# A hybrid encoder layer on one core: the second projection keeps its last input, lower weight parts stay in DRAM, the FFN weights get a memory of their own, and the last x1T store goes in four parts

## The chip, the cores and the metric

The kernel is one program on one core of a Trainium2 chip. The metric is the time of one execution on the device in microseconds (us); lower is better. The quoted time is the median of several executions.

## What is computed

One encoder layer over two requests of 256 and 2048 tokens (2304 in all) of width 1024, with shared weights, all in fp32. Cut to what matters:

```python
mod = silu(c) @ ada_w + ada_b                      # six vectors: sh1, sc1, g1, sh2, sc2, g2
h = rmsnorm(x, norm1_g) * (1 + sc1) + sh1
proj = h @ w_in                                    # 1024 -> 3*512 (hyena) + 3*512 (attention)
hy = hyena_mixer(proj[..., :1536], ...)            # short conv, two long convolutions by FFT,
                                                   # whose filters come from a small network
at = dilated_attention(proj[..., 1536:])           # 8 heads, three dilations, ALiBi
mix = concat([rmsnorm(hy, hy_out_g), rmsnorm(at, attn_out_g)]) @ w_out
x = x + g1 * mix                                   # x1
h = rmsnorm(x, norm2_g) * (1 + sc2) + sh2
gate = dwconv3(h @ ffn_w_gate, ...)                # 1024 -> 2816
x = x + g2 * ((gelu(gate) * (h @ ffn_w_up)) @ ffn_w_down)
return rmsnorm(x, final_g)
```

## The kernel before, in words

**Arithmetic.** An fp32 matmul is made of three matmuls in a shorter format: each operand is split into an upper part (a rounded copy, made by ScalarE) and a lower part (operand minus upper part, made by VectorE or GpSimd). `mm3` (L205) issues the three: upper weight by upper input (L208), upper weight by lower input (L209), lower weight by upper input (L210). All subtractions of this kind go through `sub`, so L203 stands for many tiles; they are told apart by their names. The input's parts are hThi and hTlo in the projections and hh and hl in the FFN, the weights' parts wihi and wilo there and whi and wlo here.

**Order of the work.** The stages are Python generators, and `weave` (L247) advances several of them by hand-set rates, so that one stage's matmuls stand among another's. Each engine then executes its own instructions in the order of issue. DMAs issued by SyncE (SP) stand in SP's queue in order, those issued by ScalarE in ScalarE's: a DMA that waits holds what is behind it in that queue. The program gives each DMA that SP and ScalarE issue one of eight completion counters, in turn, and a DMA waits until the one eight before it has landed.

**First projection** (`project`, L587, called from L1063). The tokens are walked in three passes of 768 own tokens (`OWN`, L477; with a few neighbours beside them, up to 772). For each pass twelve column blocks m = 0 to 11 of `w_in` are multiplied. `load_w` (L577) loads a block of 128 columns (wiraw, 512 KB, on SP, L580), casts its upper part on ScalarE (L583) and subtracts on VectorE. It does so in each pass again: the 36 block-steps load, cast and subtract 36 times. Raw, upper and lower part have two buffers each. After the matmuls ScalarE copies PSUM to the tile u (L627 or L629), a short convolution runs on GpSimd and VectorE (tile cv, L662), TensorE transposes the result (pjt, L601), and the tokens are stored by SP (L606). At block 6 of a pass `modulated` (L556) prepares the next pass's input: x is loaded on SP (L489), normed on VectorE (L519) and modulated on ScalarE and other engines (L553); at the start of the next pass `split` (L565) makes hThi (ScalarE, L571) and hTlo (VectorE).

This projection is woven with `filters` (L330): matmuls (fw, L432; fs, through `mm3`) make the filters' spectrum, VectorE forms F (L439), GpSimd forms flo and sums absolute values into acc (L454), and ScalarE's tile fae is stored on SP (d_fA, L421) 72 times. The filters end near 480 us, and the first projection runs on nearly alone until 555.

**Second projection** (L1088). The same function with m = 12 to 23 and no H given: it starts with `modulated` for pass 0, splits it, and does so again for passes 1 and 2. It is woven with the hyena convolutions. Attention's q and k of head 0 are first read after step 35 of the generator's 39 (L1097 to L1100).

**Output projection** (`output`, L1185). Blocks of 256 tokens; in each, eight column blocks m (PSUM tile om), whose results VectorE adds to x in the tile ox (L1215). At the block's end ScalarE's queue stores ox whole to x1T in DRAM (L1232, 1 MB). The previous block goes through `ffn_block` (L1236), which makes the FFN operands (tiles fV, fT) and stores them to opT in DRAM from ScalarE's queue (L1254 to L1256).

**FFN** (`output_ffn`, L1281). Both matrix products use a scheme with seven block products instead of eight; its operands are B11, T1, T2, B21, T3, B22 and T4. `operands` (L1322) loads them from opT on SP (tile hl, L1329, 289 KB each; two of the seven for the first half of the tokens are loaded ahead, beside the last output blocks), casts hh on ScalarE (L1330) and subtracts on VectorE or GpSimd. `weights7` (L1335) loads 1 MB of gate or up weights on SP (wraw, L1340), and makes the seven weight combinations from it, each with an upper part (ScalarE, L1346) and a lower part. `gate_up` runs for the two halves of the tokens; its results go to DRAM (tile cv of L1457, d_G). `down_sums` and `down_first` (L1468, L1498) prepare the down product's weights, `down` (L1520) computes it; its pool d_w holds the weights' parts dwl and dwh (L1551, L1552), and `down_first` leaves the first weights in the list W0.

**Memory.** Pools are stacked from both sides of each partition, and a pool opened where a closed one lay has its tiles wait for what was there, tile by tile (`reuse_waits="tile"`). The weights of `weights7`, `down_sums` and `down_first` lie in one pool, n_w (47,520 bytes of a partition: raw 16,384, upper 6,144, lower 6,144, the rest combinations and kept PSUM sums), which is opened after m_r, the pool of the output weights of blocks 0 to 2 (27,648 bytes), and the pools o_c and o_w of `output` are closed. The part of it that the change moves, raw and upper parts, makes 22,528 bytes.

Of the kernel before, what the change touches and what calls it, by code (L numbers as in the profile page):

```python
# [13 lines left out]
F32 = mybir.dt.float32  # L14
F32R = mybir.dt.float32r
# [6 lines left out]
P = 128  # L22
D = 1024
NT = 2304
# [165 lines left out]
class Hybrid:  # L190
# [383 lines left out]

    XB = 8

    def load_w(self, wp, src, k, tag, n=8, raws=3, bufs=2):  # L577
        nc = self.nc
        raw = wp.tile([P, 8, P], F32, tag="wraw", name=tag + "raw", bufs=raws)[:, :n]
        nc.sync.dma_start(out=raw, in_=src)  # L580
        hi = wp.tile([P, 8, P], F32R, tag="whi", name=tag + "hi", bufs=bufs)[:, :n]
        lo = wp.tile([P, 8, P], F32R, tag="wlo", name=tag + "lo", bufs=bufs)[:, :n]
        nc.scalar.copy(hi, raw)  # L583
        self.sub(nc.vector, lo, raw, hi)
        return hi, lo

    def project(self, hp, wp, w2, psp, ms, H=None):  # L587

        nc, a = self.nc, self.a
        pending = []  # L590

        def flush():
            while pending:
                pending.pop(0)()

        def to_tokens(src, dst, o0, o1, k):
            def go():
                for t0 in range(0, 6, 3):
                    ps = psp.tile([P, 512], F32, tag="pt", name="pjt", bufs=2)
                    for t in range(3):  # L600
                        nc.tensor.transpose(ps[:, t * P:(t + 1) * P], src[:, (t0 + t) * P:(t0 + t + 1) * P],  # L601
                                            self.ident)
                    if t0 == 0:
                        tt = wp.tile([P, 6, P], F32, tag="tt", name="tt", bufs=2)
                    nc.vector.tensor_copy(tt[:, t0:t0 + 3], ps[:, :3 * P].rearrange("p (t c) -> p t c", c=P))
                nc.sync.dma_start(out=dst[o0:o1].rearrange("(t p) c -> p t c", p=P)[:, :, k * P:(k + 1) * P], in_=tt)  # L606
            return go

        for p in range(3):
            if p == 0 and H is None:  # L610
                X = self.modulated(wp, 0)
            if p or H is None:
                H = [[], []]
                self.split(hp, X, H)
            yield
            o0, o1 = self.OWN[p]
            base = self.PASS[p][0][0]
            for m in ms:
                wh, wl = self.load_w(wp, a["w_in"][m], m, "wi", raws=2)
                u = wp.tile([P, 772], F32, tag="u", name="u", bufs=2)  # L620
                for (c0, n), hs in zip(self.PASS[p], H):
                    ps = psp.tile([P, 512], F32, tag="ps", name="pj")
                    for j in range(8):
                        self.mm3(ps[:, :n], wh[:, j], wl[:, j], hs[j][0], hs[j][1], j == 0, j == 7)
                    us = u[:, c0 - base:c0 - base + n]
                    if 12 <= m < 16:
                        nc.scalar.mul(us, ps[:, :n], -0.125)  # L627
                    else:
                        nc.scalar.copy(us, ps[:, :n])  # L629
                flush()  # L630
                src = u[:, o0 - base:o1 - base]
                if m < 12:
                    src = self.short_conv(w2, u, base, o0, o1, m)
                k = m % 4
                if 12 <= m < 20:
                    dst = self.qT if m < 16 else self.kT
                    nc.sync.dma_start(out=dst[k * P:(k + 1) * P, o0:o1], in_=src)
                else:
                    dst = self.tok[("hv", "x1", "x2", "", "", "av")[m // 4]]
                    pending.append(to_tokens(src, dst, o0, o1, k))  # L640
                yield
                if p < 2 and m == ms[2] and w2 is not None:
                    yield from self.input_rstd(wp, w2, psp, p + 1)
                if p < 2 and m == ms[5]:
                    X = self.modulated(wp, p + 1)
        flush()

    def short_conv(self, wp, u, base, o0, o1, m):
# [395 lines left out]
    def mixers(self):  # L1044
# [15 lines left out]
        H = [[], []]  # L1060
        for i in range(0, 8, 4):
            self.split(hp, self.modulate(X[i:i + 4], True), H)
        g = self.project(hp, wp, w2, ps, range(0, 12), H)  # L1063
        for x in (g, f, f, f):
            next(x)
        self.weave([[f, R["f"], 0], [g, R["p1"], 0]])
# [12 lines left out]
        with ExitStack() as st:  # L1079
            ap = self.pool(st, "ada2", side="left")  # L1080

            def rest():
                rows = self.ada_rows(ap)
                for i in (2, 3, 4, 5):
                    yield from self.ada_vector(i, ap, rows, 1)
                    self.ada_finish(i)

            g = self.project(hp, wp, None, ps, range(12, 24))  # L1088
            rs = rest()
            gw = [g, R["p2"], 0]  # L1090
            self.weave([h, [rs, R["ad"], 0], gw], until=rs)
# [93 lines left out]
    def output(self, psp, ap):  # L1185
# [3 lines left out]
        with ExitStack() as st:  # L1189
# [13 lines left out]
            for c0 in range(0, NT, 256):  # L1203
# [7 lines left out]
                for m in range(8):  # L1211
# [14 lines left out]
                    if m == 3 and last is not None:  # L1226
                        px, pacc, pc, pr = last
                        rs = wp.tile([P, 256], F32, tag="ors2", name="ors2", bufs=1)
                        self.rstd(psp.tile([P, 512], F32, tag="pr", name="rstd", bufs=1), [pacc], rs)
                        self.ffn_block(ap[2], px.rearrange("p (k j) t -> p k j t", k=2), rs, pc, pr, range(4))  # L1230
                    yield
                nc.scalar.dma_start(out=self.x1T[:, :, :, c0 // 2:c0 // 2 + P], in_=xe)  # L1232
                last = (xT, acc, c0, r)
            self.last = last[1:]

# [45 lines left out]
    def output_ffn(self, hy, mq, ow):  # L1281
        with ExitStack() as top, ExitStack() as s:
# [19 lines left out]
            for x in "hl":  # L1302
                for i in range(7):
                    self.hpool.setdefault((x, i), h2)
            psp = self.pool(top, "psB", bufs=8, space=PSUM)
            wp = self.pool(s, "n_w", side="right")
            gp = self.pool(s, "n_g", side="right")
            self.Gd = self.dr.tile([P, NF // 2, 7, NT // 2], F32, name="d_G")
# [26 lines left out]
    def weights7(self, wp, src):  # L1335

        nc = self.nc
        v = nc.vector
        raw = wp.tile([P, 2, 2, 4, P], F32, tag="wraw", name="wraw", bufs=2)
        nc.sync.dma_start(out=raw, in_=src)  # L1340
        A11, A12, A21, A22 = raw[:, 0, 0], raw[:, 0, 1], raw[:, 1, 0], raw[:, 1, 1]

        def parts(x, eng):
            hi = wp.tile([P, 4, P], F32R, tag="whi", name="whi", bufs=3)
            lo = wp.tile([P, 4, P], F32R, tag="wlo", name="wlo", bufs=3)
            nc.scalar.copy(hi, x)  # L1346
            self.sub(eng, lo, x, hi)
# [120 lines left out]
    def down_sums(self, wp, n):  # L1468
# [1 line left out]
        nc = self.nc  # L1470
        mp, q0 = n // 3, 4 * (n % 3)
        q1 = min(q0 + 4, NF // 2)
        raw = wp.tile([P, 2, 2, 4, P], F32, tag="wraw", name="sraw", bufs=2)[:, :, :, :q1 - q0]
        for r in range(2):
            nc.sync.dma_start(out=raw[:, r], in_=self.a["w_down"][mp, :, r, :, q0:q1])
        A11, A12, A21, A22 = raw[:, 0, 0], raw[:, 0, 1], raw[:, 1, 0], raw[:, 1, 1]
# [21 lines left out]
    def down_first(self, wp, T, W):  # L1498
# [7 lines left out]
            if q % 4 == 3:  # L1506
                yield
        yield
        raw = wp.tile([P, 2, 2, 4, P], F32, tag="wraw", name="draw", bufs=2).rearrange("p r k q m -> p (r k q) m")[:, :NQ]
        nc.sync.dma_start(out=raw, in_=self.a["w_down"][0, :, 0, 0])  # L1510
        yield
        yield
        for q0 in range(0, NQ, 4):
            k = min(4, NQ - q0)
            hi, lo = (wp.tile([P, 4, P], F32R, tag="w" + x, name="dw" + x, bufs=3)[:, :k] for x in ("hi", "lo"))
            nc.scalar.copy(hi, raw[:, q0:q0 + k])
            self.sub(nc.vector, lo, raw[:, q0:q0 + k], hi)
            W += [(hi[:, q], lo[:, q]) for q in range(k)]
# [168 lines left out]
```

## Time and profile before

| | |
|---|---|
| median of 3 runs | 3480.42 us (3474.23 to 3481.12) |
| profiled execution, its own time | 3475.7 us |
| span of that execution, first to last instruction | 3473.9 us |
| granted TensorE clock, mean of the span | 0.973 of full |
| instructions | 56,909 |

The profiled execution is one run, and every row further down comes from it. Engines are named as in the profile: PE is TensorE's matmuls, PEld its weight loads (which overlap PE), DVE is VectorE, ACT ScalarE, POOL GpSimd, SP SyncE; SPq and ACTq are the DMA queues of SyncE and ScalarE. "idle before" a group of instructions is the time its engine stood idle just ahead of them, with what ended that idle time behind an arrow. PEclk is the granted TensorE clock, 1.00 being 2.4 GHz and 0.50 being 1.2 GHz. Times in brackets such as 1904 to 1938 are us from the start of the span.

### The profile page before, as it was taken

Reading aid. Unit: us, or ns where it says so; the run is one execution under the profiler, and the core shown is the slowest. Engines: PE = TensorE matmul, PEld = TensorE weight load, DVE = VectorE, ACT = ScalarE, POOL = GpSimd, SP = SyncE. Lnnn points to the kernel's source line nnn. Section 1 sums busy time; section 2 is a strip of 40 time slices with the busy share of each in tenths; the row PEclk is TensorE's granted clock in tenths of the full one; section 3 lists DMA queues with packets and bytes.
Section 4 is the critical chain, followed back from the end, with each engine's and each line's share of the span. In section 5 each row is a group of like instructions: output and inputs, shape, how many; then the busy total and the mean of one; then the engine's idle time right before and its main releaser. Section 6 shows DMA issues by size and latency. Waiting matters only on the chain.

```text
span 3473.9 us, 56909 instructions
## 1 busy us (share of the span) xinstructions
PE 3256.6 (94%) x20926; PEld 3001.6 (86%) x20926; DVE 2459.5 (71%) x4233; ACT 1559.7 (45%) x2895; POOL 1279.4 (37%) x1018
## 2 busy tenths in 40 slices
PE   7988899989989998998898899999999999899998
PEld 4877788778867786777898899999999999899998
DVE  7988878777576667744886766776866667457657
ACT  4576753233245645455554433334433334344443
POOL 1487661133233423210544433334533335123222
PEclk9999999999999999999899999999999999999999
DMA  6454457777585867584676523445443224557555
GB/s 246 133 163 136 149 173 234 229 255 231 192 227 176 246 189 214 173 257 137 181 214 201 186 97 123 151 163 206 148 159 143 97 90 148 181 181 239 201 192 172
DMA packets 408910, 628.02 MB, mean 181 GB/s; under 512 B 29007, under 2 KB 232015, under 8 KB 402711
## 3 DMA queue, kind: packets, MB, share of 16 engines
q1 hardware_dynamic: 355472, 593.13, 52.6%
q10 hardware_dynamic: 52072, 28.40, 2.8%
q8 instruction: 166, 2.72, 0.3%
q0 software_dynamic: 1088, 2.85, 0.2%
q14 instruction: 112, 0.92, 0.1%
HBM read 419.03 MB, written 205.25 MB: 180 GB/s over the span
## 4 chain that ended last, share of the span: by engine, by line
PE 42%; DVE 5%; DMA 2%; issue 2%; ACT 1%; POOL 1%; SPq 0%; ACTq 0%; DVEq 0%; POOLq 0%
PE w L210 9%; PE w L208 9%; PE w L209 9%; PE fd L210 5%; PE fd L209 5%; PE fd L208 5%; DVE fT L1252 1%; DMA hl<-d_opT 0%; DMA d_x1T<-ox 0%; DVE ohy L1160 0%; DVE ox L1215 0%; PE om L208 0%; POOL oat L1146 0%; PE om L209 0%; PE om L210 0%
## 5 line engine op out<-in xcount | busy, mean ns | idle before, releaser
L208 PE MATMUL w<-hh,whi 128*128 128x288 f32 (+1 forms) x2464 | 735.6, 299 | 13.2 <-ACT whi L1346 8.4
L210 PE MATMUL w<-hh,wlo 128*128 128x290 f32 (+1 forms) x2464 | 733.5, 299 | 11.2 <-POOL wlo L203 7.0
L209 PE MATMUL w<-hl,whi 128*128 128x288 f32 (+1 forms) x2464 | 735.4, 299 | 2.7 <-DVE hl L203 2.7
L208 PEld LDWEIGHTS w<-hh,whi 128*128 128x128 f32 x2464 | 471.1, 191 | 14.5 <-ACT whi L1346 8.6
L210 PEld LDWEIGHTS w<-hh,wlo 128*128 128x128 f32 x2464 | 470.4, 191 | 13.2 <-POOL wlo L203 8.0
L209 PEld LDWEIGHTS w<-hl,whi 128*128 128x128 f32 x2464 | 472.7, 192 | 3.4 <-DVE hl L203 3.2
L208 PE MATMUL pj<-hThi,wihi 128*128 128x386 f32 (+1 forms) x1152 | 402.4, 350 | 12.9 <-ACT u L629 5.4
L209 PE MATMUL pj<-hTlo,wihi 128*128 128x386 f32 (+1 forms) x1152 | 399.3, 347 | 7.1 <-DVE hTlo L203 7.1
L210 PE MATMUL pj<-hThi,wilo 128*128 128x386 f32 (+1 forms) x1152 | 401.7, 349 | 0.0
L208 PE MATMUL fd<-hh,dwh 128*128 128x288 f32 x1210 | 360.3, 298 | 12.6 <-ACT dwh L1552 12.6
L210 PE MATMUL fd<-hh,dwl 128*128 128x288 f32 x1210 | 359.0, 297 | 0.0
L209 PE MATMUL fd<-hl,dwh 128*128 128x288 f32 x1210 | 357.9, 296 | 0.0
L208 PEld LDWEIGHTS pj<-hThi,wihi 128*128 128x128 f32 x1152 | 220.2, 191 | 28.3 <-issue 7.8
L208 PEld LDWEIGHTS fd<-hh,dwh 128*128 128x128 f32 x1210 | 230.0, 190 | 13.2 <-ACT dwh L1552 12.8
L209 PEld LDWEIGHTS pj<-hTlo,wihi 128*128 128x128 f32 x1152 | 220.6, 192 | 23.9 <-issue 9.7
L210 PEld LDWEIGHTS pj<-hThi,wilo 128*128 128x128 f32 x1152 | 219.9, 191 | 11.7 <-issue 7.5
L209 PEld LDWEIGHTS fd<-hl,dwh 128*128 128x128 f32 x1210 | 229.6, 190 | 0.4
L210 PEld LDWEIGHTS fd<-hh,dwl 128*128 128x128 f32 x1210 | 228.0, 188 | 0.1
L939 PEld LDWEIGHTS aOp<-aV,aPT 128*128 128x128 f32 x1408 | 184.3, 198 | 48.8 <-issue 18.4
L735 POOL TENSOR_TENSOR ht<-ht,ht 128x512 f32<-128x512 f32 x72 | 101.7, 1413 | 338.4 <-DVE ht L734 268.2
L203 POOL TENSOR_TENSOR wlo<-ws,whi 128x512 fp32r<-128x512 f32 x88 | 131.6, 1495 | 232.3 <-ACT whi L1346 225.4
L203 POOL TENSOR_TENSOR hl<-hl,hh 128x576 fp32r<-128x576 f32 (+1 forms) x66 | 116.1, 1766 | 264.6 <-ACT hh L1494 191.4
(298 smaller groups left out, 7950.1 us busy)
## 6 DMA issues: line engine op xcount, KB each, us to landing
hl<-d_G SPq DMA_DIRECT2D x154, 288.0 KB, 5.1
dwl<-d_S SPq DMA_DIRECT2D x59, 704.0 KB, 4.9
wiraw<-in_w_in SPq DMA_DIRECT2D x72, 512.0 KB, 4.6
d_G<-cv SPq DMA_DIRECT2D x42, 576.0 KB, 2.9
wraw<-in_w_gate SPq DMA_DIRECT2D x22, 1024.0 KB, 4.8
wraw<-in_w_up SPq DMA_DIRECT2D x22, 1024.0 KB, 4.9
adat<-in_ada_t SPq DMA_DIRECT2D x36, 512.0 KB, 5.6
d_fA<-fae SPq DMA_DIRECT2D x72, 256.0 KB, 2.5
```

The lines of the kernel that those rows point to most:

```text
L203: eng.tensor_tensor(out=lo, in0=x, in1=hi.bitcast(F32), op=ALU.subtract)
L208: mm(out, wh, xh, start=first, stop=False, skip_group_check=more)
L209: mm(out, wh, xl, start=False, stop=False, skip_group_check=more)
L210: mm(out, wl, xh, start=False, stop=last, skip_group_check=more)
L735: nc.gpsimd.tensor_tensor(out=t1, in0=t1, in1=t2, op=ALU.add)
L939: nc.tensor.matmul(po[:, i, hs], pe[:, hh, c], vt[:, x["v"] + c * x["vs"], hs], start=(c == 0), stop=(c == n - 1))
L1252: v.tensor_tensor(out=o, in0=x, in1=y, op=ALU.subtract)
```

## The change

It has four parts.

1. **Kept input.** `project` takes the input and the order of the passes. The first projection leaves its last split input (of pass 2) in `self.H`; the second starts with it and walks the passes as 2, 1, 0. So it modulates and splits two inputs instead of three.
2. **Lower weight parts in DRAM.** In its first pass the first projection stores each wilo to a DRAM tile (12 stores of 512 KB on SP, behind the subtraction). In passes 1 and 2 it loads wilo from there (24 loads of 512 KB on SP, issued right behind the raw load and the upper part's cast) instead of subtracting. The second projection still subtracts.
3. **A memory of their own.** Raw and upper parts of `weights7`, `down_sums` and `down_first` go to a new pool n_r, opened ahead of n_w; lower parts and the rest stay in n_w.
4. **The last x1T store.** In the last block of `output` x1T is stored by SP in four parts of 256 KB, one after each pair of column blocks; the other blocks keep ScalarE's whole store.

```diff
-    def load_w(self, wp, src, k, tag, n=8, raws=3, bufs=2):
+    def load_w(self, wp, src, k, tag, n=8, raws=3, bufs=2, kept=None, known=False):
         ...
         nc.scalar.copy(hi, raw)
-        self.sub(nc.vector, lo, raw, hi)
+        if known:
+            nc.sync.dma_start(out=lo.bitcast(F32), in_=kept)
+        else:
+            self.sub(nc.vector, lo, raw, hi)
+            if kept is not None:
+                nc.sync.dma_start(out=kept, in_=lo.bitcast(F32))
         return hi, lo

-    def project(self, hp, wp, w2, psp, ms, H=None):
+    def project(self, hp, wp, w2, psp, ms, H, passes):
         ...
-        for p in range(3):
-            if p == 0 and H is None:
-                X = self.modulated(wp, 0)
-            if p or H is None:
+        lows = self.dr.tile([len(ms), P, 8, P], F32, name=f"d_wlo{ms[0]}") if w2 is not None else None
+        for p, after in zip(passes, passes[1:] + (None,)):
+            if p != passes[0]:
                 H = [[], []]
                 self.split(hp, X, H)
+            self.H = H
             yield
             ...
-                wh, wl = self.load_w(wp, a["w_in"][m], m, "wi", raws=2)
+                wh, wl = self.load_w(wp, a["w_in"][m], m, "wi", raws=2, kept=None if lows is None else lows[m - ms[0]],
+                                     known=lows is not None and p != passes[0])
                 ...
-                if p < 2 and m == ms[2] and w2 is not None:
-                    yield from self.input_rstd(wp, w2, psp, p + 1)
-                if p < 2 and m == ms[5]:
-                    X = self.modulated(wp, p + 1)
+                if after is not None and m == ms[2] and w2 is not None:
+                    yield from self.input_rstd(wp, w2, psp, after)
+                if after is not None and m == ms[5]:
+                    X = self.modulated(wp, after)
 # mixers
-        g = self.project(hp, wp, w2, ps, range(0, 12), H)
+        g = self.project(hp, wp, w2, ps, range(0, 12), H, (0, 1, 2))
-            g = self.project(hp, wp, None, ps, range(12, 24))
+            g = self.project(hp, wp, None, ps, range(12, 24), self.H, (2, 1, 0))
 # output
+                    if c0 + 256 == NT and m % 2:
+                        nc.sync.dma_start(out=self.x1T[:, m - 1:m + 1, :, c0 // 2:c0 // 2 + P], in_=xe[:, m - 1:m + 1])
                     yield
-                nc.scalar.dma_start(out=self.x1T[:, :, :, c0 // 2:c0 // 2 + P], in_=xe)
+                if c0 + 256 < NT:
+                    nc.scalar.dma_start(out=self.x1T[:, :, :, c0 // 2:c0 // 2 + P], in_=xe)
 # output_ffn
+            self.rp = self.pool(s, "n_r", side="right")
             wp = self.pool(s, "n_w", side="right")
 # weights7, and the raw tiles of down_sums and down_first in the same way
-        raw = wp.tile([P, 2, 2, 4, P], F32, tag="wraw", name="wraw", bufs=2)
+        raw = self.rp.tile([P, 2, 2, 4, P], F32, tag="wraw", name="wraw", bufs=2)
         ...
-            hi = wp.tile([P, 4, P], F32R, tag="whi", name="whi", bufs=3)
+            hi = self.rp.tile([P, 4, P], F32R, tag="whi", name="whi", bufs=3)
             lo = wp.tile([P, 4, P], F32R, tag="wlo", name="wlo", bufs=3)
```

## Rows read from the trace of the kernel before

**Rows 1.** The page's first part: busy time of each engine, its share of the span, and its instructions.

```profile
PE 3256.6 (94%) x20926; PEld 3001.6 (86%) x20926; DVE 2459.5 (71%) x4233; ACT 1559.7 (45%) x2895; POOL 1279.4 (37%) x1018
```

**Rows 2.** The table by stage: the stretch and its length, then busy time (and instructions) of PE, PEld, DVE, ACT and POOL, the granted clock PEclk, the DMA engines' busy share, and the GB/s that they moved.

```profile
211.00:480.00 269.00, 243.31 (x1235) 216.22 (x1235) 234.24 (x241) 196.51 (x342) 210.74 (x140) 0.97 0.47 146
480.00:555.00 75.00, 72.56 (x410) 69.11 (x408) 59.15 (x70) 31.66 (x48) 26.13 (x16) 1.00 0.77 240
552.00:563.00 11.00, 7.58 (x29) 7.26 (x28) 10.06 (x14) 7.24 (x13) 0.00 (x0) 0.69 0.76 246
...
1904.00:1938.00 34.00, 20.02 (x95) 18.49 (x94) 20.84 (x22) 14.66 (x28) 14.88 (x12) 0.70 0.90 314
1938.00:2408.00 470.00, 468.85 (x3483) 468.29 (x3482) 330.61 (x485) 170.62 (x325) 178.45 (x146) 1.00 0.38 134
...
2938.00:2973.00 35.00, 17.60 (x108) 16.66 (x108) 24.72 (x32) 10.03 (x13) 13.55 (x11) 0.80 0.47 175
```

**Rows 3.** Instructions grouped by line, VectorE, 211 to 555: count, busy time, mean ns of one, then the idle time just before them and what ended most of it.

```profile
L439 DVE TENSOR_TENSOR F<-fw,fE 64x512 f32<-64x512 f32 x114 | 78.4, 688 | 26.7 <-POOL flo L203 16.5 <-PE fw L433 5.9 <-ACT fE L430 1.5
L203 DVE TENSOR_TENSOR wilo<-wiraw,wihi 128x1024 fp32r<-128x1024 f32 x25 | 41.7, 1670 | 0.8 <-ACT wihi L583 0.4
```

**Rows 4.** The same grouping, TensorE's matmuls, 211 to 480.

```profile
L209 PE MATMUL pj<-hTlo,wihi 128*128 128x386 f32 (+1 forms) x279 | 96.4, 346 | 5.6 <-DVE hTlo L203 5.6
L432 PE MATMUL fw<-W3s,Hh 128*128 128x512 f32 x55 | 23.6, 429 | 12.8 <-DVE F L439 12.7
L209 PE MATMUL fs<-flo,fkt 128*128 128x512 f32 x56 | 23.5, 419 | 2.0 <-POOL flo L203 2.0
L601 PE MATMUL pjt<-ident,cv 128*128 128x128 f32 x106 | 16.9, 283 | 3.7 <-DVE cv L662 3.7
```

**Rows 5.** The same grouping, GpSimd, 211 to 480.

```profile
L454 POOL TENSOR_TENSOR acc<-acc,fabs 128x512 f32<-128x512 f32 x60 | 92.9, 1549 | 28.7 <-ACT fabs L453 13.6 <-PE fw L433 10.9 <-DVE x L519 2.5
L203 POOL TENSOR_TENSOR flo<-F,fhi 128x512 fp32r<-128x512 f32 x56 | 90.5, 1621 | 3.3 <-ACT fhi L414 3.3
```

**Rows 6.** Waits of SP's DMA queue, 211 to 555: the line that waits and what it waited for, then us in total, times, and the longest in us.

```profile
SPq L421 <- ACT fae L420: 107.5, 38, 8.5
SPq L580 <- DVE wilo L203: 53.3, 22, 6.3
```

**Rows 7.** DMA issues, 211 to 555: destination and source, queue, count, KB each, and the median us from issue to landing.

```profile
d_fA<-fae SPq DMA_DIRECT2D x64, 256.0 KB, 2.9
wiraw<-in_w_in SPq DMA_DIRECT2D x25, 512.0 KB, 4.3
```

**Rows 8.** The table by stage for the instructions that touch the tile wilo alone: stretch, length, busy time (and count) of PE (the matmuls that read it or stand in its chains), PEld and DVE (the subtractions), then clock, DMA share and GB/s of the stretch.

```profile
211.00:480.00 269.00, 95.34 (x279) 53.43 (x279) 29.46 (x18) 0.97 0.47 146
480.00:555.00 75.00, 39.06 (x116) 21.62 (x115) 10.28 (x7) 1.00 0.77 240
```

**Rows 9.** Instructions grouped by line, ScalarE, 529 to 562 (the hand-over to the second projection).

```profile
L553 ACT ACTIVATE x<-x,mod,ga 128x386 f32<-128x386 f32 x14 | 9.0, 701 | 8.4 <-DVE x L519 8.4
L571 ACT CAST hThi<-x 128x772 fp32r<-128x772 f32 (+1 forms) x8 | 6.6, 837 | 1.2 <-PE pj L210 1.1
```

**Rows 10.** The same, VectorE, 529 to 562.

```profile
L519 DVE TENSOR_TENSOR x<-x,rs 128x772 f32<-128x772 f32 x8 | 8.5, 1087 | 0.0
L203 DVE TENSOR_TENSOR hTlo<-x,hThi 128x772 fp32r<-128x772 f32 (+1 forms) x8 | 8.0, 1027 | 0.0
```

**Rows 11.** The same, TensorE's matmuls, 480 to 562.

```profile
L208 PE MATMUL pj<-hThi,wihi 128*128 128x384 f32 (+1 forms) x121 | 42.7, 356 | 3.4 <-ACT u L627 3.4
```

**Rows 12.** The timeline of ScalarE's queue near the FFN's start: start in us, length in us, queue, line, what was issued.

```profile
1905.46 6.58 ACTq L1232 DMA_DIRECT2D d_x1T<-ox  x1
```

**Rows 13.** Waits of SP's DMA queue, 1860 to 1935, as in rows 6.

```profile
SPq L1340 <- PE om L210: 25.2, 2, 22.7
...
SPq L1329 <- DMA d_opT<-fT: 6.0, 1, 6.0
SPq L1329 <- DMA d_opT<-fV: 4.4, 1, 4.4
...
SPq L1329 <- DMA d_x1T<-ox: 2.9, 1, 2.9
```

**Rows 14.** What the DMA engines moved from 1899 to 1935, and one group of DMA issues in that stretch, as in rows 7.

```profile
DMA packets 9410, 11.19 MB, mean 311 GB/s; under 512 B 448, under 2 KB 6592, under 8 KB 9152
...
hl<-d_opT SPq DMA_DIRECT2D x20, 289.0 KB, 5.9
```

**Rows 15.** The chain of waits that ended last, 1904 to 1940: start, length, what it was.

```profile
1905.46 16.20 DMA d_x1T<-ox
```

**Rows 16.** Instructions grouped by line, TensorE's matmuls, 1904 to 1938.

```profile
L209 PE MATMUL w<-hl,whi 128*128 128x290 f32 (+1 forms) x29 | 11.8, 408 | 2.7 <-DVE hl L203 2.7
L208 PE MATMUL w<-hh,whi 128*128 128x290 f32 (+1 forms) x32 | 11.8, 390 | 11.3 <-ACT whi L1346 8.4 <-ACT hh L1330 2.9
```

**Rows 17.** The timeline of VectorE near the FFN's start: start, length, engine, line, instruction; in brackets the idle time before it and what ended it.

```profile
1904.85 0.47 DVE L1215 SCALAR_TENSOR_TENSOR ox<-om,mod,ox 128x256 f32<-128x256 f32 x1
...
1912.78 0.69 DVE L203 TENSOR_TENSOR wlo<-wraw,whi 128x512 fp32r<-128x512 f32 x1 [4.63 <-ACT whi L1346]
```

**Rows 18.** The chain of waits at the start of the down product, 2950 to 2975, as in rows 15.

```profile
2957.79 3.31 DMA d_G<-cv
...
2961.26 4.16 DMA dwl<-d_S
```

More of the change, by code (lines that the diff above doesn't have):

```diff
@@ L1472, in down_sums @@
         q1 = min(q0 + 4, NF // 2)
-        raw = wp.tile([P, 2, 2, 4, P], F32, tag="wraw", name="sraw", bufs=2)[:, :, :, :q1 - q0]
+        raw = self.rp.tile([P, 2, 2, 4, P], F32, tag="wraw", name="sraw", bufs=2)[:, :, :, :q1 - q0]
         for r in range(2):
@@ L1508, in down_first @@
         yield
-        raw = wp.tile([P, 2, 2, 4, P], F32, tag="wraw", name="draw", bufs=2).rearrange("p r k q m -> p (r k q) m")[:, :NQ]
+        raw = self.rp.tile([P, 2, 2, 4, P], F32, tag="wraw", name="draw", bufs=2).rearrange("p r k q m -> p (r k q) m")[:, :NQ]
         nc.sync.dma_start(out=raw, in_=self.a["w_down"][0, :, 0, 0])
@@ L1514, in down_first @@
             k = min(4, NQ - q0)
-            hi, lo = (wp.tile([P, 4, P], F32R, tag="w" + x, name="dw" + x, bufs=3)[:, :k] for x in ("hi", "lo"))
+            hi, lo = (y.tile([P, 4, P], F32R, tag="w" + x, name="dw" + x, bufs=3)[:, :k]
+                      for x, y in (("hi", self.rp), ("lo", wp)))
             nc.scalar.copy(hi, raw[:, q0:q0 + k])
```

## The prediction

> **What bounds the kernel now.** The page's first part comes first: TensorE is busy for 94% of the span [rows 1], so a stage gains only where TensorE sits idle or runs at its lower clock. The table by stage says where that is [rows 2]. The long FFN loop (1938 to 2408: 469 of 470 us busy) has no idle time to give. Of what the change touches, four places have some: the first projection beside the filters (211 to 480: 243 of 269 us busy, clock 0.97, VectorE busy for 234 of 269), the hand-over to the second projection (near 555), the start of the FFN (1904 to 1938: 20 of 34 us busy, clock 0.70) and the start of the down product (2938 to 2973). At each the reader looks for what ended TensorE's idle time.
>
> In 211 to 480 nearly all of that idle time was ended by VectorE: 12.7 us before the filter matmuls, 5.6 before matmuls that wait for hTlo, 3.7 before transposes [rows 4]. At the FFN's start it is one wait of 8.4 us for the first weight part, then four short ones for operands, 5.6 us together [rows 16]. The chain there runs through the last x1T store: 16.20 us from its issue to its landing [rows 15]. ScalarE's queue needed 6.58 us to issue that store alone [rows 12], and the first weight parts (ACT whi, DVE wlo at 1912.78 [rows 17]) stood behind it.
>
> **Part 1, the kept input.** In the second projection one of three sets of loading, normalizing, modulating and splitting goes, with eight x loads. At the hand-over ScalarE spent 6.6 us on 8 hThi casts and 9.0 us on modulations [rows 9], VectorE 8.0 us on 8 hTlo and 8.5 us on 8 normings [rows 10]. Nearly all of it lies beside TensorE, which is busy for 72.6 of the 75 us before [rows 2]. What shows is one idle piece of 3.4 us, a PSUM copy standing behind those modulations [rows 11]. The clock fell to half just behind it; 6.8 us at half speed cost about 3.4 us (an estimate from that stretch's granted clock, 0.69 over 11 us in 552 to 563) [rows 2]. Ends: 0, if another wait takes its place, and 6.8. I take 5. Walking the passes as 2, 1, 0 changes which tokens of q, k and v come last; attention reads head 0's q and k after step 35 of 39, four column blocks behind their stores, so this costs nothing unless those stores are late by a whole pass step.
>
> **Part 2, the lower parts from DRAM.** In passes 1 and 2 of the first projection 24 subtractions leave VectorE. A mean one takes 1.67 us [rows 3]: 40 us, of which 18, or 30 us, lie in 211 to 480 [rows 8]. In come 12 stores and 24 loads of 512 KB, all on SP. A load of the same size and queue lands 4.3 us after its issue [rows 7]. It can start when its buffer is free, that is when TensorE is through with column block m-2, and is needed by the third matmul of block m. Between lies one block: 269/18 = 14.9 us beside the filters, 75/7 = 10.7 us after them [rows 8]. SP is in order; its longest wait before a filter store was 8.5 us [rows 6]. 8.5 + 4.3 = 12.8 fits into 14.9 but not into 10.7, so in the worst step of the tail TensorE waits 2 us, for 6 or 7 steps 14 us; but no filter store is left there, so I take 0 to 3. The 18.9 MB are 37 GB/s over 505 us (50 to 555), beside 146 to 240 GB/s [rows 2]; the 12 stores wait for the same subtraction that the next raw load already waits for (53.3 us of SP's waits [rows 6]), and nobody waits for them.
>
> What do 30 us of VectorE buy? At most the 22 us of idle time that VectorE ended [rows 4] and the clock behind it: 3% of 269 us is 8. At least nothing, since GpSimd is busy for 211 of the 269 us [rows 2], and VectorE itself waited 16.5 us for GpSimd's flo [rows 3] and then delivers no faster. VectorE falls from 87% to 76% busy; its queue gets shorter but doesn't vanish. I take a third of 30, with 2 off for late loads: 8. Ends: +14 (tail loads late, nothing gained) and -30.
>
> **Part 3, the weights' own memory.** By the tile sizes, n_w took the last 47,520 bytes of a partition, and its first raw buffer lay on the output weights of blocks 5 and 6; so SP held both loads until TensorE was through with them: 25.2 us in two waits for om [rows 13]. In n_r (22,528 bytes) raw and upper parts lie on the weights of blocks 0 to 2, which are free some 15 us earlier. Both loads (1 MB each) move ahead of the rush. At the start of the down product the new layout puts W0's lower parts under the second and third buffer of d_w. That costs nothing, since the first load there waits for the last G store until 2961.10 anyway (3.31 us of DMA, then 4.16 of loading [rows 18]), and W0 is done by then; without that cover it would cost W[2]'s load, up to 4.16 us.
>
> **Part 4, the x1T store.** Three quarters leave up to 18 us earlier, when their pairs are done; the last one leaves SP just after VectorE's last ox at 1904.85 [rows 17]. Nearest row for 256 KB: 2.9 us to landing [rows 7]; with 1 MB of fT and the operand loads beside it I take 5 to 7, so it lands near 1911 instead of 1921.66. That matters because the program hands its DMAs eight completion counters in turn: operand loads of hl waited 2.9 us for x1T, 6.0 for fT and 4.4 for fV, whose data they don't need [rows 13]. Behind the new stores on SP stand those 20 loads.
>
> Between 1899 and 1935 the DMA engines carry 11.19 MB at 311 GB/s [rows 14], nearly saturated. 2 MB of weights and 0.75 MB of x1T leave that stretch: 8.4 MB, 27 us instead of 36 us. So the operands come 9 us earlier, and the first product starts 7 to 8 us earlier (VectorE's first wlo after 1905.3 instead of 1912.78). Ceiling: 95 matmuls in 34 us need, at 470/3483 = 0.135 us each [rows 2], 12.8; 21 us are lost today. TensorE will still wait for the operands after two steps. I take 9.5. Ends: 3 and 15.
>
> Here a rule speaks against the change. The row shows a store whose issue alone holds ScalarE's queue for 6.58 us [rows 12]. The Trainium skill (DMA: Bandwidth & Descriptors, "Issuing engines are not separate DMA queues") says that a DMA run from another engine's queue shares the same 16 DMA engines and saves only issue time, usually small; its "Rules for kernel authors" want 1 MiB per DMA. By these the fourth part would give about 0, and the sum would lose most of the 9.5. This trace disagrees as to "small", with 6.58 us; it agrees on the shared engines, at 311 GB/s.
>
> **Sum.** 5 + 8 + 9.5 = 22.5 us off the profiled execution's 3475.7 us: 3453. That execution is 4.7 us under the median of the three runs (3480.4; they span 6.9 us, which is the 0.2% that a measurement can tell). On the median it is 3458; I say 3456.
>
> **Rivals.**
> GpSimd paces the filters: part 2 gives nothing. For it: the 16.5 us above, and flo and acc take 183 of 269 us on GpSimd [rows 5]. Against: TensorE's idle time was ended by F, a VectorE product, six times as often as by flo (12.7 against 2.0 us). 14.5 us off: 3463 on the same scale.
> The FFN's start gives nothing: the operands stay bound by transfers, the last quarter queues behind fT. For it: the saturated stretch. Against: 2.75 MB leave it. Parts 1 and 2 alone: 3465. With both rivals only part 1 is left: 3473.
> Slower, by one mechanism: the lower-part loads come late in every step. The place is TensorE's third matmul of a block; the load stands on SP behind filter stores that wait for ScalarE's fae (107.5 us in 38 waits [rows 6]). It decides from a delay on SP of 14.9 - 4.3 = 10.6 us on, where the longest seen is 8.5. At 2 us in each of 24 steps 48 us come, part 2's 8 us go: 3456 + 56 = 3512 at full price, 3488 at half. Against it: the mean wait is 107.5/38 = 2.8 us.
> It does more than I allow: all VectorE idle time and clock in 211 to 480 (30 us) and 15 at the FFN: 3430.
> That a part doesn't do what it says (the raw loads stay behind the x1T parts on in-order SP) ends in the second rival.
>
> **Chances.** Forecast 0.47, GpSimd 0.20, FFN start 0.12, both 0.08, more than forecast 0.07, slower 0.06. The range 3434 to 3473 holds the first four and half of the fifth, cut where their edges lie outside. Faster by over 0.2% 0.83, within 0.11 (both rivals, and the weak edge of each), slower 0.06.
>
> **What would show it.** Right: wilo disappears from VectorE in passes 1 and 2, TensorE idle before fw falls from 12.7 to under 8 us and 211 to 480 shrinks by about 8; no idle time before pj ended by DMA wilo; no ACT issue of 6 us near 1905, the first wlo before 1907, operand loads ending 8 to 10 us sooner after the last om; the stretch before the down product as before. Wrong: idle time before pj's third matmul ended by DMA, or SP's wilo loads waiting over 10 us; a filter stretch as long as before with VectorE less busy; gate weights still loaded after the last om block.

## The result and the profile after

The changed kernel takes 3433.9 us (median of four; 3431.2 to 3442.1) against 3477.8 us: ratio 0.9878 (95% interval 0.9856 to 0.9899), 35 to 50 us less. The forecast was 3456; the time lies just at the lower edge of the range (3434 to 3473). The gain was twice the 22 us forecast.

Both profiled executions by stage follow, first before, then after. Each boundary is the same matmul in both: pass 1 begins; last fw; first projection ends; three blocks into the second projection; its end; last aOp; last om; one eighth of the gate and up products; end. Columns as in [rows 2].

```profile
195.00:464.80 269.80, 241.22 (x1222) 214.12 (x1221) 235.55 (x243) 198.82 (x345) 212.82 (x139) 0.97 0.48 149
464.80:538.20 73.40, 70.81 (x397) 66.43 (x396) 56.93 (x59) 33.32 (x51) 33.16 (x24) 1.00 0.66 203
538.20:575.40 37.20, 33.78 (x169) 31.26 (x168) 32.56 (x43) 16.41 (x28) 7.94 (x4) 0.91 0.83 270
575.40:984.00 408.60, 382.28 (x1887) 328.40 (x1887) 277.29 (x385) 114.43 (x182) 102.70 (x66) 0.99 0.67 218
984.00:1633.40 649.40, 610.85 (x3452) 489.33 (x3450) 423.26 (x1336) 347.64 (x804) 179.63 (x198) 0.96 0.70 205
1633.40:1904.40 271.00, 239.64 (x1888) 234.46 (x1888) 212.70 (x434) 141.37 (x304) 124.33 (x105) 0.94 0.66 197
1904.40:2051.80 147.40, 132.32 (x927) 130.77 (x927) 107.05 (x151) 62.55 (x117) 59.86 (x45) 0.93 0.45 154
2051.80:3473.80 1422.00, 1381.03 (x10198) 1375.46 (x10196) 947.09 (x1332) 539.56 (x904) 491.77 (x382) 0.99 0.46 161
```

```profile
195.00:440.80 245.80, 230.95 (x1207) 209.12 (x1206) 210.27 (x225) 198.73 (x343) 206.68 (x142) 0.99 0.63 200
440.80:515.90 75.10, 74.27 (x422) 70.19 (x422) 51.98 (x57) 27.82 (x44) 31.15 (x25) 1.00 0.76 252
515.90:549.20 33.30, 33.30 (x169) 29.19 (x168) 26.41 (x38) 5.53 (x9) 7.20 (x3) 1.00 0.72 239
549.20:947.20 398.00, 378.40 (x1882) 327.55 (x1881) 269.27 (x375) 116.14 (x189) 101.93 (x66) 1.00 0.69 222
947.20:1596.80 649.60, 605.30 (x3446) 488.93 (x3445) 419.86 (x1331) 348.09 (x803) 180.12 (x196) 0.96 0.69 202
1596.80:1868.40 271.60, 239.86 (x1890) 234.84 (x1890) 212.88 (x434) 142.06 (x305) 124.02 (x105) 0.93 0.67 208
1868.40:2008.70 140.30, 129.18 (x928) 126.92 (x927) 107.53 (x151) 62.66 (x116) 59.62 (x46) 0.96 0.41 140
2008.70:3430.10 1421.40, 1381.62 (x10197) 1376.12 (x10196) 944.81 (x1332) 539.18 (x904) 495.98 (x382) 0.98 0.46 161
```

Subtract the lengths: beside the filters 24.0 us less, the tail 1.7 more, the hand-over 3.9 less, the rest of the second projection 10.6 less, the FFN's start 7.1 less, all else within 0.6. Beside the filters VectorE's busy time fell by 25.3 us and the stretch by 24.0.

The rows that answer to [rows 4] (TensorE, beside the filters). First one of the kernel before over the same stage, 195 to 464.8, since [rows 4] has a narrower window; then the changed kernel, 195 to 441:

```profile
L432 PE MATMUL fw<-W3s,Hh 128*128 128x512 f32 x57 | 24.5, 430 | 16.1 <-DVE F L439 16.0
```

```profile
L209 PE MATMUL pj<-hTlo,wihi 128*128 128x386 f32 (+1 forms) x271 | 93.1, 344 | 2.3 <-DVE hTlo L203 2.3
L432 PE MATMUL fw<-W3s,Hh 128*128 128x512 f32 x57 | 23.8, 417 | 8.0 <-DVE F L439 7.8
L209 PE MATMUL fs<-flo,fkt 128*128 128x512 f32 x57 | 22.7, 398 | 0.0
L607 PE MATMUL pjt<-ident,cv 128*128 128x128 f32 x98 | 15.7, 277 | 4.6 <-DVE cv L669 4.6
```

Over the whole stage, idle time before fw that VectorE ended fell from 16.0 to 7.8 us, before hTlo's readers from 6.2 to 2.3; before transposes it grew from 3.5 to 4.6. The loaded lower parts came in time: the page has 0.3 us of TensorE's idle time ahead of all 1152 matmuls of that kind in both projections.

```profile
L210 PE MATMUL pj<-hThi,wilo 128*128 128x386 f32 (+1 forms) x1152 | 396.5, 344 | 0.3
```

### The profile page after: what moved, and what is told of

It reads as the page before. It is cut to its first block, busy times and chain, and to the rows that moved or that the text cites. A ratio compares the mean times of both kernels' runs of the same rounds, so it can differ in the third digit from the quotient of the medians.

```text
span 3430.1 us, 56856 instructions
## 1 busy us (share of the span) xinstructions
PE 3238.3 (94%) x20926; PEld 2995.7 (87%) x20926; DVE 2408.7 (70%) x4193; ACT 1544.0 (45%) x2871; POOL 1271.6 (37%) x1018
## 3 DMA queue, kind: packets, MB, share of 16 engines
q0 software_dynamic: 1088, 2.85, 0.3%
## 4 chain that ended last, share of the span: by engine, by line
PE 43%; DVE 4%; DMA 2%; issue 1%; ACT 1%; POOL 1%; ACTq 0%; SPq 0%; DVEq 0%; POOLq 0%
PE w L210 9%; PE w L208 9%; PE w L209 9%; PE fd L210 5%; PE fd L209 5%; PE fd L208 5%; DVE fT L1262 1%; DMA hl<-d_opT 0%; DVE ohy L1167 0%; DVE hl L203 0%; PE om L208 0%; POOL oat L1153 0%; DVE ox L1222 0%; PE om L209 0%; PE om L210 0%
## 5 line engine op out<-in xcount | busy, mean ns | idle before, releaser
L208 PE MATMUL fd<-hh,dwh 128*128 128x288 f32 x1210 | 359.8, 297 | 12.5 <-ACT dwh L1564 12.5
L208 PEld LDWEIGHTS pj<-hThi,wihi 128*128 128x128 f32 x1152 | 219.1, 190 | 23.4 <-issue 5.0
```

What stands on the lines that cost most here:

```text
L208: mm(out, wh, xh, start=first, stop=False, skip_group_check=more)
```

## The experiments

All ratios are to the kernel before, with 95% intervals; stage times come from each kernel's one profiled execution. Such an execution carries some 5 us of chance: e3 and e4 run the same instructions in the same order as the kernel before up to the output projection, and still led it by 5.6 and 4.6 us at the end of the second projection. The nine kernels without part 2 end their last fw between 459.5 and 465.9 us, the four with it and without added subtractions between 440.3 and 446.5.

**Each part alone** (the diff's own lines).

e1, part 2 alone: 

> The kernel before with part 2 alone (wilo stored once and loaded in passes 1 and 2). Theory A, VectorE sets the pace beside the filters: what leaves VectorE there (about 17 subtractions of 1.7 us, 29 us) leaves the time nearly one for one; the last matmul fs comes 24 to 29 us earlier than the 503.1 us of before, and the whole is 22 to 30 us faster (3448 to 3456). Rival B, GpSimd sets the pace there and the gain needs the other parts: at most 10 us (3468 or more), VectorE's idle time beside the filters rising by the rest. Rival C, the part also shortens the second projection, by the other alignment of its streams: over 32 us.

Measured: 0.9931 (0.9919 to 0.9943), 24 us. Last fs at 477.2 instead of 503.1, last fw 23.4 earlier: theory A. The tail to the end of the first projection then took 80.1 us instead of 73.4, with 3.0 us of idle time before a transpose (cv) and 2.5 before an fs matmul (frn), none before wilo's readers. By the end of the second projection this execution led by 15.6 us; attention, which part 2 doesn't touch, then took 643.3 us instead of 649.4, so not all of the 24 us can be placed in part 2's own stages.

e2, part 1 alone: 

> The kernel before with part 1 alone (kept input, passes 2, 1, 0). Theory A, only the hand-over is worth something: 3 to 6 us faster, all of it between the first projection's last block and the second's first ones; the rest of the second projection as before within 2 us. Rival B, the whole second projection gains, since one set of loading, norming, modulating and splitting is taken out of a stretch that waits for the convolutions' operands: 12 to 16 us faster, and the 37 us by which the changed kernel leads at the end of the second projection are 22 of part 2 and 15 of this.

Measured: 0.9945 (0.9932 to 0.9958), 19 us; hand-over 35.3 us, the rest of the second projection 393.4 instead of 408.6. Theory A fell; rival B's size holds roughly, its reason is tested by e6 and e7.

e3, part 4 alone: 

> The kernel before with part 4 alone (last x1T store in four parts on SP). Theory A, it was ScalarE's queue, held for 6.58 us by the issue of the one store, that kept the first weight parts back: the first product starts 5 to 8 us earlier after the last om (8.4 us after it before, 0 in the changed kernel). Rival B, the weights' raw load, which waits for om of the last block, is as late: 0 to 3 us faster, with the first upper part waiting for the raw load.

Measured: 0.999 (0.9978 to 1.0002). In the profile the first product starts 3.9 us after the last om (8.4 before), and the stretch to its first eighth takes 144.9 us instead of 147.4. The start came 4.5 us earlier, short of theory A's 5; the whole can't be told from no change, and the first upper part waits for its raw load (1.74 us), as rival B had it.

e4, part 3 alone: 

> The kernel before with part 3 alone (raw and upper weight parts in a pool of their own). Theory A, the raw loads come early, but the upper part's cast still stands behind the 6.58 us issue on ScalarE's queue: 0 to 3 us faster. Rival B, the 2 MB that leave the rush bring the operands forward: 4 to 8 us faster, with ScalarE casting before it issues the store.

Measured: 0.9966 (0.9954 to 0.9978), 12 us. The first product starts 0.2 us before the last om has ended, and the stretch takes 139.2 us, 8.2 less. Rival B, at the upper end of its 4 to 8 us. ScalarE's timeline in this kernel:

```profile
1893.10 0.62 ACT L1347 CAST whi<-wraw 128x512 fp32r<-128x512 f32 x1 [1.26 <-DMA wraw<-in_w_gate]
...
1903.61 1.38 ACTq L1232 DMA_DIRECT2D d_x1T<-ox  x1
```

The first weight part was cast 10 us before the store was issued, and the issue of the same whole store took 1.38 us, not 6.58 [rows 12]. In the kernel before, SP had issued 2 MB of weight loads in the 4 us ahead of it; with these gone, the issue is short. The same kernel issues eight more whole stores of this size, one in each earlier block, in 0.53 to 3.62 us each, so 6.58 is not what the queue takes for such a store.

**e8, the changed kernel without part 4** (the whole store, from ScalarE's queue). 

> The changed kernel without part 4 (the last x1T store goes whole from ScalarE's queue again). Theory A, parts 3 and 4 remove the same wait, so that part 4 adds nothing to part 3: ratio to before 0.986 to 0.989 as the changed kernel, the first product starting 0 us after the last om and its loss before the loop as before within 1 us. Rival B, they add up: 3 to 5 us slower than the changed kernel (ratio 0.989 to 0.990), and the first eighth of the product ends 3 to 5 us later after the last om.

Measured: 0.9883 (0.9868 to 0.9899); the stretch takes 138.7 us, against 140.3 with part 4. Theory A, by the stretch: with part 3 in place part 4 adds nothing. (The ratio's interval alone would not exclude rival B.) ScalarE's timeline again has the short issue:

```profile
1861.74 0.62 ACT L1354 CAST whi<-wraw 128x512 fp32r<-128x512 f32 x1 [2.64 <-DMA wraw<-in_w_gate]
1870.87 1.38 ACTq L1239 DMA_DIRECT2D d_x1T<-ox  x1
```

**The parts don't add up.** Alone, parts 2, 1 and 3 gain 24, 19 and 12 us, 55 together; at once, with part 4, they gain 44. The gap of 11 us is about as large as its uncertainty (some 10 us from the intervals), and where it goes isn't shown.

**e5, VectorE's work put back, the loads kept**, on the changed kernel.

```diff
             nc.sync.dma_start(out=lo.bitcast(F32), in_=kept)
+            for h in range(2):
+                spare = wp.tile([P, 4, P], F32R, tag="wsp", name="wsp", bufs=1)
+                self.sub(nc.vector, spare, raw[:, 4 * h:4 * h + 4], hi[:, 4 * h:4 * h + 4])
```

> The changed kernel, whose passes 1 and 2 of the first projection also do the subtraction on VectorE again, in two halves into a spare tile that nobody reads; the stores and loads of the lower parts stay. Theory A, VectorE's work itself sets the pace beside the filters and the 18.9 MB cost nothing: the last fw matmul comes back to 460 to 470 us (440.8 in the changed kernel, 464.8 before), the whole is 20 to 28 us slower than the changed kernel (ratio to before 0.994 to 0.996). Rival B, TensorE gained because the lower part no longer stands in VectorE's order ahead of its matmuls (a latency), not because VectorE has less to do: the last fw stays under 450 and the ratio near 0.988. Rival C, the loads themselves cost something that VectorE's relief hid: last fw later than 475, ratio 0.998 or more.

Measured: last fw at 463.2 (464.8 before, 440.8 changed): theory A for the stage. Its row, VectorE's spare subtractions and TensorE's wait for F in it:

```profile
195.00:463.20 268.20, 242.22 (x1230) 215.03 (x1229) 250.43 (x262) 199.17 (x343) 215.11 (x142) 0.97 0.59 186
```

```profile
L203 DVE TENSOR_TENSOR wsp<-wiraw,wihi 128x512 fp32r<-128x512 f32 x35 | 39.8, 1138 | 1.7 <-ACT wihi L584 1.1
L432 PE MATMUL fw<-W3s,Hh 128*128 128x512 f32 x57 | 25.1, 441 | 15.5 <-DVE F L439 15.2 <-DVE W3s L203 0.2
```

DMA carries 186 GB/s instead of 149 and the stretch is as long as before, so no cost of the loads shows there. The price was not one for one: against the changed kernel VectorE's busy time rose by 40.2 us and the stretch by 22.4. VectorE was busy for 14.9 us more than in the kernel before, in a stretch that is no longer. The whole came out less clear: ratio 0.9903 (0.9889 to 0.9918), 10 us slower than the changed kernel by medians and not the 20 to 28 expected; the profiled execution, the slowest of five, is 18 us slower than the changed kernel's. For the whole, theory A's range was missed, and what the stage took in the other four executions isn't shown.

**e6 and e7, order and kept input apart.** Both are the kernel before with other passes: e6 walks 2, 1, 0 and makes all inputs anew; e7 keeps the input and walks 2, 0, 1. The cut is against part 1; its first four lines are e6's alone.

```diff
+            if H is None:
+                X = self.modulated(wp, p)
-            if p != passes[0]:
+            if p != passes[0] or H is None:
-  range(12, 24), self.H, (2, 1, 0))
+  range(12, 24), None, (2, 1, 0))        # e6
+  range(12, 24), self.H, (2, 0, 1))      # e7
```

> The kernel before, whose second projection walks the passes as 2, 1, 0 but makes all three inputs anew. Theory A, part 1 gains by the work that it takes out: no change (ratio 0.998 to 1.002), 36/72 to 72/72 of the projections' matmuls in 441 to 447 us as before. Rival B, the order gains, since it moves what is stored last: ratio 0.994 to 0.997, that stretch in 428 to 433 us as in the kernel with part 1 alone.

Measured: 0.9966 (0.9951 to 0.998), 12 us.

> The kernel before with the kept input, but passes 2, 0, 1 instead of 2, 1, 0. Theory A (the work taken out): as the kernel with part 1 alone, ratio 0.993 to 0.996, the second projection's stretch in 428 to 433 us. Rival B (the order): ratio 0.998 to 1.001, stretch in 441 to 447 us.

Measured: 1.0002 (0.999 to 1.0014). Rival B both times: the order 2, 1, 0 gains. Hand-over, then the rest of the second projection, of e6 and then of e7 (with its attention):

```profile
536.10:573.30 37.20, 32.17 (x170) 28.64 (x169) 33.39 (x43) 16.25 (x28) 8.02 (x4) 1.00 0.89 277
573.30:971.10 397.80, 381.77 (x1886) 330.10 (x1886) 272.67 (x381) 117.05 (x190) 98.46 (x66) 0.99 0.68 222
```

```profile
539.10:569.50 30.40, 30.40 (x163) 28.22 (x163) 22.01 (x32) 5.28 (x9) 4.62 (x3) 1.00 0.80 255
569.50:975.00 405.50, 383.70 (x1887) 330.46 (x1886) 271.42 (x380) 115.08 (x182) 103.84 (x67) 0.99 0.67 218
975.00:1632.00 657.00, 611.41 (x3452) 490.75 (x3451) 423.86 (x1336) 347.88 (x804) 179.23 (x198) 0.96 0.70 202
```

In e7, with the kept input, the hand-over is shorter (30.4 us, not 37.2); in e6, with the order, the rest is (397.8, not 408.6). The hand-over's length is a weak measure, since the weaving put 163 to 180 matmuls into it: over all kernels it took 30.4 to 38.8 us (38.8 in e5) with the input kept and 36.1 to 37.7 without. TensorE's idle time in it says more: 0 to 2.3 us in the six kernels that keep the input, 1.8 to 5.0 in the eight that don't. In e7 attention took 657.0 us instead of 649.4 and gave the gain back; whether the order 2, 0, 1 does that isn't shown, since no run walks it with all inputs made anew.

**e9, e11, e12, why the order?** In the kernel before, attention's first pieces of q and k are taken up in the middle of the second projection: near 820, with thirteen of its 36 column blocks still to come, and not after step 35 of 39, as the section on the kernel and the prediction have it. ScalarE waits 7.25 us there for q's load, and GpSimd 4.2 us for ScalarE's cast of k. e9, on the kernel before, loads whole rows, which come later (the first cast of q at 896):

```diff
+        if head == 0:
+            for t, src in ((Ql, self.qT), (Ks, self.kT)):
+                for d in range(2):
+                    nc.sync.dma_start(out=t[64 * d:64 * d + 64].bitcast(F32), in_=src[hr])
...
-                for d in range(2):
+                for d in range(2 if head else 0):
```

> The kernel before (passes 0, 1, 2, three inputs made anew), whose attention loads q and k of head 0 in four whole rows instead of four pieces of 576 tokens each, so that no piece can be taken up before the last pass has stored its k. Theory A, the reversed order gained because the first two pieces no longer come in the middle of the second projection, where ScalarE, VectorE and GpSimd stood waiting for their loads ahead of the convolutions' operands (before: 7.25 us on ScalarE and 4.2 us on GpSimd near 820): 54/72 to 72/72 of the projections' matmuls falls from 226 to 232 us to 218 to 224 us, ratio 0.996 to 0.999. Rival B, the order gained in another way: that stretch stays at 226 us or more.

Measured: 1.0005 (0.9994 to 1.0016), the stretch named 232.5 us. Theory A fell. e11 and e12 are e6 with other orders.

> The kernel before with the second projection's passes as 1, 2, 0, all three inputs made anew. Open is why the order 2, 1, 0 alone gained 12 us while late q and k gained nothing. Theory A, what counts is that pass 0 comes last: ratio 0.995 to 0.998 as with 2, 1, 0. Theory B, no rule, the streams only fall differently against each other: a ratio that is off from both 1.000 and 0.9966, or 1.000 here while 0, 2, 1 moves.

Measured: 0.9994 (0.9982 to 1.0005).

> The same with passes as 0, 2, 1. Theory A (pass 0 last counts): no change, 0.999 to 1.001. Theory B (no rule): it moves by more than 0.2% either way.

Measured: 1.0006 (0.9995 to 1.0017). That pass 0 comes last is not the reason either. The rest of the second projection took 393 to 400 us in the six kernels with 2, 1, 0 (changed, e2, e5, e6, e8, e10) and 404 to 411 in the eight with another order. What TensorE waits for there, in the kernel before and in the changed one:

```profile
L727 PE MATMUL hs2z<-hx,htab 128*128 128x512 f32 x50 | 25.7, 595 | 2.7 <-DMA hx<-d_hA 2.7
L692 PE MATMUL hs<-hS,hf 128*128 128x512 f32 x36 | 16.0, 444 | 12.5 <-POOL hS L203 12.5
```

```profile
L734 PE MATMUL hs2z<-hx,htab 128*128 128x512 f32 x50 | 25.7, 596 | 1.7 <-DMA hx<-d_hA 1.7
L699 PE MATMUL hs<-hS,hf 128*128 128x512 f32 x36 | 15.5, 429 | 6.5 <-POOL hS L203 6.5
```

The waits for hS, an operand of the convolutions that is split on GpSimd, fell from 12.5 to 6.5 us. Since e11 has them at 5.8 us and gains nothing, they aren't the whole reason. Nor is idle time as a whole: in e11's row TensorE is idle for 20.8 us, in the changed kernel's for 19.6, but its matmuls are busy for 384.1 us against 378.4, at a granted clock of 0.98 against 1.00.

```profile
576.50:981.40 404.90, 384.09 (x1886) 330.40 (x1886) 270.97 (x381) 117.04 (x190) 100.11 (x66) 0.98 0.67 218
```

Why just this order gains stays open.

**e10, a try at more**, on the changed kernel:

```diff
-                    nc.vector.tensor_copy(tt[:, t0:t0 + 3], ...)
+                    copy = nc.scalar.copy if t0 and w2 is not None else nc.vector.tensor_copy
+                    copy(tt[:, t0:t0 + 3], ...)
-                for _ in self.operands(H, b, range(7) if b else range(2, 7)):
+                for _ in self.operands(H, b, (0, 1, 2, 5, 4, 6, 3)[0 if b else 2:]):
```

> The changed kernel with two additions. One: in the first projection the second PSUM copy of each transposed block (tile tt) goes from VectorE to ScalarE. Theory A, VectorE still sets the pace beside the filters (210 of 246 us busy, ScalarE 199): about 9 us leave it, the last fw matmul comes 4 to 8 us earlier than 440.8. Rival B, the pace has gone over to ScalarE and GpSimd: 0, or up to 5 us later. Two: the FFN operands are loaded in the order in which the products use them (T2, B21, T3, B22, T4 instead of T2, T4, T3, B21, B22). If the operands' order is what the first product waits for (hl, 5.3 us of TensorE's idle time), 2 to 5 us are gained there and 0 to 4 at the second half's start. Together ratio to before 0.983 to 0.987, against 0.9878.

Measured: 3432.7 us, 0.9871 (0.9851 to 0.989), not to be told from the changed kernel. The last fw came 5.7 us later (446.5), so rival B for the first addition, a little beyond its 5 us; at the FFN's start the second gained 0.7 us, less than expected. VectorE lost 9 us of copies, and its short convolution took 12.8 us more. The changed kernel comes first, then e10, then one of two instructions of e10 (8.23 and 5.79 us) that make up 11 of the 12.8 us; GpSimd ran six instructions back to back beside the first:

```profile
L666 DVE SCALAR_TENSOR_TENSOR cv<-u,c_short,cv 128x768 f32<-128x768 f32 (+2 forms) x18 | 25.7, 1428 | 3.9 <-POOL cv L663 3.6
```

```profile
L667 DVE SCALAR_TENSOR_TENSOR cv<-u,c_short,cv 128x768 f32<-128x768 f32 (+2 forms) x18 | 38.5, 2140 | 3.2 <-POOL cv L664 2.8
344.85 8.23 DVE L667 SCALAR_TENSOR_TENSOR cv<-u,c_short,cv 128x768 f32<-128x768 f32 x1 [0.62 <-POOL cv L664]
```

## Why the prediction was right or wrong

**Sign and places** were right: all three places on which the sum was put got shorter, and no rival that made it slower came true.

**Part 2, forecast 8, measured 22** (24.0 less the tail's 1.7; 24 alone). The step that failed is "I take a third of 30". I took GpSimd's 211 busy us of 269 for a limit, and VectorE's waits for flo for slack. Neither held: the stretch gave back nearly all that VectorE lost (24.0 of 25.3 us), and e5's profiled execution, with the work returned, was as long as before. The two engines weren't independent either: without the subtractions GpSimd's own busy time fell from 212.8 to 206.7 us. The bound of -30 was the better reading of 87% busy, though e5 shows some slack too. Not separated is whether VectorE's queue as such set the pace or its turns with GpSimd (last section): e5 brings back both, and e10, which took 9 us of copies off VectorE, gained nothing. The lower-part loads were late by nothing (forecast: 2 us off).

**Part 1, forecast 5, measured 3.9 at the hand-over**, in line with the mechanism named (idle time 3.4 us before, 0 after; clock 0.91 and 1.00), but in one execution and within its chance; e6 had the clock at 1.00 there with all inputs made anew, and 5.0 us idle. The argument that the order 2, 1, 0 costs nothing took q and k to be read after step 35 (the trace has the first pieces near 820), looked at nothing else, and left out that a new order can also gain. It is worth 12 us by itself (e6), the 10.6 us in the rest of the second projection that I had no term for.

**Parts 3 and 4, forecast 9.5, measured 7.1 by the first eighth of the products** (8.6 at the first product). The size held, the share-out did not. The issue of 6.58 us was a consequence of the rush and not a price of ScalarE's queue: in the stretch part 3 alone gets all of it, part 4 alone about 2.5 us. Here the Trainium skill (DMA: Bandwidth & Descriptors, "Issuing engines are not separate DMA queues") says that another issuing engine saves only a usually small issue time. Once the weights had left, e4 and e8 agree with 1.38 us; I had set the row of 6.58 us against the rule without asking what made it long. The loads of the operands did come sooner, but by 6.4 us (the last was issued 17.5 us after the last om instead of 23.9) and not by 8 to 10.

**Rivals.** "GpSimd paces the filters" (0.20), in the form that part 2 gives nothing, is refuted by e1 and e5, "the FFN's start gives nothing" (0.12) by e4. The case with the nearest time, "more than forecast" (0.07, 3430), had all of VectorE's idle time and more at the FFN; the time agrees better than its terms do (22 for 30, 7 for 15, and 11 from the order). That the time still lies in the range is in part luck: part 2 gave 14 us more than its term, the order 11 us that had none, and both carried it to the edge.

## What to carry to other kernels

Where an engine is busy for seven eighths of a stretch and ends nearly all of TensorE's idle time, cost its removed work well above a third: here 0.56 (e5 against the changed kernel) to 0.95 (the change) of its busy time came back as time. Its waits for a partner that works in turn with it need not be slack. Before a long DMA issue is booked on its queue, look at what was issued just ahead of it. Where several streams are woven, try a reordering by itself: it can be worth as much as the saving it was made for, and an order that looks as good can give nothing.

## What the runs showed of the hardware

VectorE's time for the same instruction went with what GpSimd did beside it. The subtraction wilo (1024 elements, both operands in SBUF) took 1280 ns in the mean from 51 to 195 us, where GpSimd was busy for 66.5 of 144 us, and 1719 ns beside the filters, where it was busy for 212.8 of 269.8. GpSimd's share alone doesn't set it: in the second projection (575.4 to 984), with 102.7 of 408.6 us, the mean is 1414 ns. One by one it is clearer. Of the 70 in the kernel before from 51 to 984 us, the 25 beside which GpSimd ran nothing took 1.21 to 1.23 us each; the 45 beside one of its instructions took up to 2.85 us, 1.62 in the mean. One of each, the second with GpSimd's instructions beside it:

```profile
403.81 1.23 DVE L203 TENSOR_TENSOR wilo<-wiraw,wihi 128x1024 fp32r<-128x1024 f32 x1
246.49 2.35 DVE L203 TENSOR_TENSOR wilo<-wiraw,wihi 128x1024 fp32r<-128x1024 f32 x1
246.45 1.30 POOL L454 TENSOR_TENSOR acc<-acc,fabs 128x512 f32<-128x512 f32 x1
247.71 2.29 POOL L203 TENSOR_TENSOR flo<-F,fhi 128x512 fp32r<-128x512 f32 x1
```

F, which reads PSUM and is as long each time, took 688 ns beside the filters in the kernel before, the changed kernel, e5 and e10. The Trainium skill (SBUF — State Buffer, "SBUF: two separate sides") has VectorE and GpSimd take turns at a shared pair of SBUF ports, held for a whole instruction, when VectorE has two inputs there and GpSimd reads SBUF. These rows agree; no run here tested it by itself. It fits e10 too, where the convolution that grew longer has two inputs in SBUF; that taking away copies that read PSUM caused it isn't shown, since GpSimd was about as busy as in the changed kernel (207.4 and 206.7 us).
